# Series of small float32 products, whole and in column groups, after the last product of a two-layer hybrid model

## The chip, the cores and the metric

The kernel runs on one core of one Trainium2 chip. The core has five engines with queues of their own: TensorE (matrix products, its weight loads shown apart), VectorE (DVE), ScalarE (ACT), GpSimd (POOL) and SyncE (SP, which here issues most transfers). The metric is the device time of one execution in microseconds. The time before is the median of 2 runs, 1101.77 us; a profile was taken of one further execution.

## The reference

A model of two layers over 256 tokens of width 1024, with a memory of 256 tokens, all in float32. Each layer has four blocks, each closed by a layer normalization:

```python
for l in range(DEPTH):                      # 2
    h = layer_norm(ALPHA * h + 0.5 * swiglu(h, ffn1_gate[l], ffn1_up[l], ffn1_down[l]), ...)
    z = h @ w_in[l]
    cb, cc, ch, rq, rf, ri, rg, pu = jnp.split(z, split_at, axis=-1)
    y_conv = short_gated_conv(ch, cb, cc, conv_w[l])
    y_rec = hgrn2(rq, rf, ri, rg, lbs[l], rec_norm_g[l])
    y_pool = multiscale_pool(pu, pool_w[l], pool_scale[l])
    mix = jnp.concatenate([y_conv, y_rec, y_pool], axis=-1) @ w_out[l]
    h = layer_norm(ALPHA * h + mix, ...)
    h = layer_norm(ALPHA * h + cross_attn(h, mem, ca_q[l], ca_k[l], ca_v[l], ca_o[l]), ...)
    h = layer_norm(ALPHA * h + 0.5 * swiglu(h, ffn2_gate[l], ffn2_up[l], ffn2_down[l]), ...)
```

The two feed-forward blocks (1024 to 2816 and back) are most of the arithmetic. The change adds nothing to what is computed: the output is `h` after the second layer, as before.

## The kernel before

All data has 128 partitions. The tokens are two tiles of 128 (`NT = 2`), the width 1024 is eight tiles of 128 (`NK = 8`). The activations stand transposed in SBUF as `xT`, of shape 128 x 8 x 2 x 256: for each of the eight blocks of the width first the high parts of 256 tokens, then their low parts. `mT` is the same for the memory. Both are float32r, a form of float32 that TensorE multiplies in one pass with fewer bits. `split` (lines 60 to 62) makes high and low parts: ScalarE rounds a float32 tile to float32r, and VectorE subtracts that from the source. A product of float32 matrices is then three float32r products, high with high, high with low and low with high, all issued by `product` at line 106.

Weights come in blocks of 1 MB through `load` (line 76 issues the transfers on SyncE's queue) and are split the same way into `whi` and `wlo`.

Some smaller products use plain float32, not float32r: the blocks of the recurrence (lines 688, 711, 754, 764 and 765), the pooling's weights (line 816, 256 columns streamed) and the transposes by an identity (170, 254, 827, 888). At the start of the first feed-forward block, line 430 issues products of a zeroed tile into a PSUM tile `blank` that nothing reads; the helper `busy` is called with 5, 1 and 2.

PSUM has one pool with two tags, `acc` and `dn`, of four buffers each, one bank of 128 x 512 float32 a buffer. `acc(shape, tag)` takes the next buffer of a tag. A `dn` quadruple holds the four results (two token tiles, two halves of the width) of a block that returns to the width.

The last block is the second layer's `ffn(l, "ffn2", 3, ..., last=True)`. It ends in `finish`, which closes the two token tiles one after the other. For the second one the last half of the width is done in two pieces of 256 columns with an `acc` buffer each; VectorE adds a piece to `h` (line 309), takes statistics (317, 319, 321), GpSimd takes the power (322), VectorE normalizes (325, 329), and the output goes out from line 334 on the queues of SyncE and ScalarE. These steps follow the last matrix product of the program.

Most of the order of work is made by a planner that knows each engine's instructions and their dependencies. Inside `tc.manual_schedule(engines={...})` the named engines take their instructions in the order in which they are written. Line 966 of the profile is the end of the program, where SyncE waits for each engine and queue and all engines meet.

Of the kernel before, what the change touches and what calls it, by code (L numbers as in the profile page):

```python
# [8 lines left out]
F32 = mybir.dt.float32  # L9
# [5 lines left out]
E = mybir.EngineType  # L15
PSUM = bass.MemoryType.PSUM

P = 128
# [923 lines left out]
        pend = ffn(l, "ffn2", 3, pend, last=l == DEPTH - 1)  # L942


# [1 line left out]
_INS = [  # L946
    "x", "mem", "ffn1_gate", "ffn1_up", "ffn1_down", "w_in", "conv_w", "rec_lb", "rec_norm_g", "pool_w",
# [22 lines left out]
```

## Time and profile before

| what | us |
|---|---|
| time, median of 2 runs (1101.72 to 1101.82) | 1101.77 |
| the profiled execution, its time | 1101.39 |
| the profiled execution, from first to last instruction (span) | 1099.7 |
| VectorE busy | 834.5 |
| ScalarE busy | 566.2 |
| TensorE, products of line 106 with `whi` and `xT` into `acc`, 1312 of 512 columns | 394.9 |

The profile is of one execution. A row of the timeline gives start, length, engine (PE is a matmul, PEld a weight load, a q behind an engine its queue), source line, operation, output and inputs, shape and count; neighbouring instructions of one kind are merged, and the length then runs from the first start to the last end. Matmuls are pipelined: a row's recorded length is longer than the step from one start to the next. "128*128" are the rows and columns of the array that are used; "128x512" is the streamed operand. The shapes name both float32 and float32r as f32.

### The profile page before, as it was taken

The numbers are of one execution on the slowest core, as the hardware profiler recorded it, in microseconds if no ns is written. First come the engines' busy times: TensorE is split into PE (matmuls) and PEld (weight loads), VectorE is DVE, ScalarE is ACT, GpSimd is POOL, SyncE is SP. The second block draws the span as 40 slices with busy tenths as digits, with TensorE's granted clock in tenths as the row PEclk, the third lists the DMA queues.
The fourth block names the chain that finished last, engine by engine and source line by source line (L and its number), as shares of the span: only waits on it lengthen the run. The fifth ranks groups of instructions, "written<-read, shape, count | busy, mean of one in ns | idle before, by whom it ended". The sixth has DMA issues, their size and how long they took to land.

```text
span 1099.7 us, 14684 instructions
## 1 busy us (share of the span) xinstructions
PE 1089.5 (99%) x5667; PEld 968.6 (88%) x5667; DVE 834.5 (76%) x1089; ACT 566.2 (51%) x767; POOL 63.9 (6%) x112
## 2 busy tenths in 40 slices
PE   9999999999999999999999999999999999999997
PEld 7888888999899888888888888899998998888886
DVE  6678678998788777666687655699988877766665
ACT  6465454665457355444455445456564654554450
POOL 9600000000000000000000000000000000000000
PEclk9999999999999999999999999999999999999999
DMA  9987665744484396766488676656545645876651
GB/s 322 295 279 242 211 220 165 253 143 153 157 277 168 110 301 214 236 214 218 153 269 266 211 221 210 220 181 203 175 133 191 229 154 180 264 240 216 215 168 38
DMA packets 115749, 228.64 MB, mean 208 GB/s; under 512 B 5536, under 2 KB 38592, under 8 KB 110560
## 3 DMA queue, kind: packets, MB, share of 16 engines
q1 hardware_dynamic: 113888, 225.33, 62.9%
q0 software_dynamic: 1216, 1.20, 0.4%
q10 hardware_dynamic: 576, 1.18, 0.3%
q8 instruction: 44, 0.72, 0.3%
q14 instruction: 25, 0.20, 0.1%
HBM read 216.15 MB, written 1.05 MB: 198 GB/s over the span
## 4 chain that ended last, share of the span: by engine, by line
PE 98%; DVE 1%; issue 0%; DMA 0%; ACT 0%; DVEq 0%
PE acc L106 64%; PE dn L106 30%; PE acc L170 1%; PE dn L711 1%; DMA h<-in_x_dram 0%; PE dn L765 0%; PE dn L688 0%; DVE wlo L62 0%; PE dn L754 0%; PE dn L764 0%; PE dn L888 0%; PE acc L888 0%; DVE yr L772 0%; DVE h L329 0%; DVE h L325 0%
## 5 line engine op out<-in xcount | busy, mean ns | idle before, releaser
L62 DVE TENSOR_TENSOR wlo<-raw,whi 128x1024 fp32r<-128x1024 f32 (+1 forms) x396 | 474.1, 1212 | 187.7 <-ACT whi L61 176.2
L61 ACT CAST whi<-raw 128x1024 fp32r<-128x1024 f32 (+1 forms) x396 | 402.9, 1041 | 344.9 <-PE dn L106 160.1
L106 PE MATMUL acc<-whi,xT 128*128 128x512 f32 x1312 | 394.9, 379 | 0.0
L106 PEld LDWEIGHTS acc<-whi,xT 128*128 128x128 f32 x1312 | 247.8, 189 | 35.0
L106 PE MATMUL acc<-wlo,xT 128*128 128x512 f32 x656 | 248.6, 379 | 0.0
L106 PE MATMUL acc<-xT,whi 128*128 128x512 f32 x576 | 141.9, 382 | 0.0
L106 PEld LDWEIGHTS acc<-wlo,xT 128*128 128x128 f32 x656 | 124.0, 189 | 17.5
L106 PE MATMUL dn<-whi,ah 128*128 128x512 f32 x346 | 131.5, 380 | 0.0
L106 PE MATMUL dn<-wlo,ah 128*128 128x512 f32 x346 | 131.1, 379 | 0.0
L106 PE MATMUL dn<-whi,al 128*128 128x512 f32 x346 | 131.1, 379 | 0.0
L106 PEld LDWEIGHTS acc<-xT,whi 128*128 128x128 f32 x576 | 104.2, 190 | 11.2
L106 PE MATMUL dn<-whi,xT 128*128 128x512 f32 x288 | 88.2, 382 | 0.0
L106 PEld LDWEIGHTS acc<-xT,wlo 128*128 128x128 f32 x576 | 75.5, 191 | 3.9
L106 PE MATMUL acc<-xT,wlo 128*128 128x256 f32 x576 | 75.9, 275 | 0.0
L106 PEld LDWEIGHTS dn<-whi,al 128*128 128x128 f32 x346 | 65.4, 189 | 9.2
L106 PEld LDWEIGHTS dn<-wlo,ah 128*128 128x128 f32 x346 | 65.4, 189 | 9.2
L106 PEld LDWEIGHTS dn<-whi,ah 128*128 128x128 f32 x346 | 65.4, 189 | 9.2
L322 POOL TENSOR_TENSOR rs<-rs,nhalf 128x1 f32<-128x1 f32 x16 | 15.0, 935 | 855.5 <-DVE rs L321 855.5
L411 DVE STREAM_TRANSPOSE square<-dealt 128x512 f32<-128x512 f32 x40 | 63.4, 1656 | 0.5 <-DMA dealt<-sg 0.5
L106 PEld LDWEIGHTS dn<-whi,xT 128*128 128x128 f32 x288 | 54.4, 189 | 7.9 <-ACT whi L61 0.5
L106 PE MATMUL dn<-wlo,xT 128*128 128x512 f32 x144 | 54.8, 380 | 0.3 <-DVE wlo L62 0.3
L315 DVE SCALAR_TENSOR_TENSOR h<-h,dn 128x512 f32<-128x512 f32 x31 | 21.2, 684 | 33.9 <-PE dn L106 33.9
(204 smaller groups left out, 992.1 us busy)
## 6 DMA issues: line engine op xcount, KB each, us to landing
raw<-in_ffn_up_dram SPq DMA_DIRECT2D x44, 1024.0 KB, 5.1
raw<-in_ffn_down_dram SPq DMA_DIRECT2D x44, 1024.0 KB, 5.2
raw<-in_ffn_gate_dram SPq DMA_DIRECT2D x42, 1024.0 KB, 5.1
raw<-in_w_in_dram SPq DMA_DIRECT2D x24, 1024.0 KB, 5.0
dealt<-sg SPq DMA_DIRECT2D x80, 128.0 KB, 3.3
raw<-in_ca_k_dram SPq DMA_DIRECT2D x8, 1024.0 KB, 4.9
raw<-in_w_out_dram SPq DMA_DIRECT2D x8, 1024.0 KB, 4.9
raw<-in_ca_v_dram SPq DMA_DIRECT2D x8, 1024.0 KB, 5.1
```

The lines of the kernel that those rows point to most:

```text
L61: nc.scalar.copy(hi, src)
L62: nc.vector.tensor_tensor(lo, src, hi.bitcast(F32), op=ALU.subtract)
L106: nc.tensor.matmul(o, w, x, start=start, stop=stop)
L170: nc.tensor.transpose(pt[:, k, :], src[:, (4 * j + k) * P : (4 * j + k + 1) * P], unit)
L315: nc.vector.scalar_tensor_tensor(v, v, ALPHA / scale, sums(y[i][n]), op0=ALU.mult, op1=ALU.add)
L322: nc.gpsimd.tensor_tensor(rs, rs, nhalf[:, 0:1], op=ALU.pow)
L411: nc.vector.transpose(d.rearrange("p k (i b) -> p b k i", b=4), x[:, :, i, :].rearrange("p b (j k) -> p b k j", k=4))
L711: nc.tensor.matmul(o[:, hh], kc[:, hh, :], view(qf, hh * P + c, (other - c, 2), (2 * c, a), (1, c)), start=True, stop=True,)
```

## The change

Behind the loop over the layers three helpers and one block of hand-ordered TensorE work are added:

```diff
         pend = ffn(l, "ffn2", 3, pend, last=l == DEPTH - 1)
 
+    x1, m1 = (a.rearrange("p k h s -> p (k h s)") for a in (xT, mT))
+
+    def small(o, m, n, count, groups=None):
+        for i in range(count):
+            g = i % (P // m) if groups is None else groups[i % len(groups)]
+            w = x1[:, 512 * (i % 7) + m * g : 512 * (i % 7) + m * g + m].bitcast(F32)
+            x = m1[:, 512 * (i % 6) + n * g : 512 * (i % 6) + n * g + n].bitcast(F32)
+            nc.tensor.matmul(o[g * m : g * m + m, 0:n], w, x, start=True, stop=True)
+
+    def large(o, count, n=512):
+        for i in range(count):
+            x = m1[:, 512 * (i % 6) : 512 * (i % 6) + n]
+            nc.tensor.matmul(
+                o[:, 0:n], x1[:, 512 * (i % 7) : 512 * (i % 7) + P], x.rearrange("p (h c) -> p c h", h=2),
+                start=True, stop=True,
+            )
+
+    with tc.manual_schedule(engines={E.PE}):
+        o = acc((P, 512))
+        d = [acc((P, 512), "dn") for _ in range(2)]
+        large(o, 16)
+        small(o, 128, 128, 24)
+        small(o, 64, 64, 24)
+        small(o, 64, 64, 24, (0,))
+        small(o, 64, 128, 24)
+        small(o, 32, 32, 24)
+        small(o, 32, 64, 24)
+        small(o, 32, 128, 24)
+        small(o, 128, 64, 24)
+        small(o, 64, 64, 24)
+        for form in ((128, 128, 4), (64, 64, 8), (32, 32, 16), (64, 64, 16), (128, 64, 4)):
+            for r in range(4):
+                small(d[r % 2], *form)
+                large(o, 8)
+        large(o, 4)
+        large(o, 16, 256)
```

`small` multiplies `count` times. Each product loads `m` columns of the transposed activations as weights, all 128 rows deep, streams `n` columns of the transposed memory past them, and writes `m` partitions and `n` columns of PSUM. With `m` of 64 or 32 the products take turns among the two or four groups of `m` columns (group `g` writes partitions `g * m` onward); with `groups=(0,)` all stay in the first. Both operands are read as float32. `large` multiplies in float32r with 128 columns loaded and 512, or 256, streamed, as `product` does. In the text a small product of `m` loaded and `n` streamed columns is called m x n; nine series of 24 stand in a row, and then five forms are repeated four times each with eight large products behind every repetition. Nothing reads `o` or `d`, and every product starts its own sum.

## The prediction

> **What bounds the kernel now.** The page was read first: its engine table, then its chain that ended last.
>
> ```profile
> span 1099.7 us, 14684 instructions
> ...
> PE 1089.5 (99%) x5667; PEld 968.6 (88%) x5667; DVE 834.5 (76%) x1089; ACT 566.2 (51%) x767; POOL 63.9 (6%) x112
> ...
> PE 98%; DVE 1%; issue 0%; DMA 0%; ACT 0%; DVEq 0%
> ```
>
> TensorE is busy for 99% of the span and carries 98% of the chain. There is no idle TensorE time in mid-kernel that could take new products; what it leaves, 1099.7 - 1089.5 = 10.2 us, lies mostly behind its last product. So the end was read next, in the timeline, with the chain of waits in the same stretch (start, length, engine and line) and the rows of the last line of the program.
>
> ```profile
> 1079.98 8.20 PE dn L106 x38
> 1088.18 4.03 PE acc L106 x36
> ```
>
> ```profile
> 1091.82 0.19 PEld L106 LDWEIGHTS acc<-whi,al 128*128 128x128 f32 x1
> 1091.93 0.28 PE L106 MATMUL acc<-whi,al 128*128 128x256 f32 x1
> 1092.24 0.42 DVE L309 TENSOR_TENSOR h<-h,acc 128x256 f32<-128x256 f32 x1 [1.12 <-PE acc L106]
> ...
> 1096.02 0.35 ACTq L334 DMA_DIRECT2D out_dram<-h  x1
> ```
>
> ```profile
> L966 SPq EVENT_SEMAPHORE  x12: 17/28/28, 1096.8 to 1099.6; - x12
> ...
> L966 SPq DRAIN  x3: 7/7/7, 1098.8 to 1099.1; - x3
> L966 PEldq DRAIN  x2: 13/1106/2200, 1090.0 to 1099.2; - x2
> ```
>
> The last matrix product starts at 1091.93. Behind it come the last normalization on VectorE, the output's transfers, and from 1096.8 the closing waits of the sync queue, one per engine and queue, then drains and the end at 1099.7. TensorE's queue drains from 1090.0 for 2200 ns, so until 1092.2, and then waits for the others. The first closing drain of the sync queue is at 1098.8. If TensorE ends last, what follows it is this closing alone, 1099.7 - 1098.8 = 0.9 us.
>
> **The change, part by part.** It removes and moves nothing. It adds 408 small float32 products and 196 large float32r ones, in an order written by hand, on TensorE alone. No engine reads them, so nobody waits for them but the end of the program. Their inputs were finished long before. The nine rows that follow hold all prices: six of the timeline, two of the groups by shape and one of line 430.
>
> ```profile
> 215.51 1.95 PE L688 MATMUL dn<-q,k 128*128 128x128 f32 x16
> 217.22 0.46 PE L106 MATMUL acc<-whi,xT 128*128 128x512 f32 x1
> 217.51 0.38 PE L106 MATMUL acc<-wlo,xT 128*128 128x512 f32 x1
> ```
>
> ```profile
> 266.38 1.03 PE L816 MATMUL acc<-win,wpool 128*128 128x256 f32 x4
> ```
>
> ```profile
> 7.62 0.19 PEld L106 LDWEIGHTS dn<-wlo,xT 128*128 128x128 f32 x1 [0.62 <-DVE wlo L62]
> 7.62 0.48 PE L106 MATMUL dn<-wlo,xT 128*128 128x512 f32 x1 [0.32 <-DVE wlo L62]
> ```
>
> ```profile
> L688 PE MATMUL dn<-q,k 128*128 128x128 f32 x32 | 3.9, 275 | 0.0
> ...
> L816 PE MATMUL acc<-win,wpool 128*128 128x256 f32 x8 | 2.1, 379 | 0.0
> ```
>
> ```profile
> L430 PE MATMUL dn<-kTh x8: 396/628/796, 1.5 to 6.4; 128*128 128x512 f32 x8
> ```
>
> *How many instructions.* Line 688 issues 8 products per layer, 16 in both, and has 32 records: a float32 product is two pairs of a weight load and a matmul. So 408 small products are 816 pairs; a large float32r product is one.
>
> *Large products.* 512 columns: 8.20 / 38 = 0.2158 us. 256 columns: 4.03 / 36 = 0.112. There are 16 + 20 x 8 + 4 = 180 of the first and 16 of the second: 38.8 + 1.8 = 40.6 us.
>
> *Price of a small pair by its streamed columns.* At 128 columns line 688 gives (1.95 - 0.275) / 15 = 0.1117 us, at 256 line 816 gives (1.03 - 0.379) / 3 = 0.217 (a merged row runs from its first start to its last end, so one recorded length, 275 or 379 ns, comes off). The slope is 0.823 ns a column with 6.4 ns fixed; my estimate is 0.0591 us at 64 columns and 0.0327 at 32.
>
> *Price of a pair by its loaded columns.* No load of under 128 columns is in the trace. The product at 7.62 found the array empty: it lasted 0.48 where its kind lasts 0.38, so a bare load of 128 columns is about 0.10 to 0.11 us, close to the 0.1117 of the pair. In the stream that load costs nothing: the load at 1091.82 starts under a product still running, and the next product starts 0.11 later. For fewer columns the bounds are a load in proportion (0.055 us at 64, 0.0275 at 32) and one that doesn't shrink (0.11). I take the proportion, because the streaming side of the same array shows it, and so a pair costs by the larger of its two widths.
>
> *Sum.* Largest width 128: 40 products of 128x128, 24 each of 64x128 and 32x128, 40 of 128x64, together 128, so 256 pairs x 0.1117 = 28.6 us. Width 64: 168 of 64x64 (72 in the series, 32 + 64 in the repeated forms) and 24 of 32x64, so 384 x 0.0591 = 22.7. Width 32: 88 products, 176 x 0.0327 = 5.8. Small products: 57.1 us; with the large ones 97.7.
>
> *Switches.* Between series the kind of product changes 29 times to or from column groups. The nearest row is the change of type behind line 688: 16 pairs and one large product fill 217.51 - 215.51 = 2.00 us, and 16 x 0.1117 + 0.2158 is 2.003, so that change is free. The upper bound is a pipeline emptied each time, the recorded 0.275 less 0.112, plus a bare load of 0.11: 0.27 x 29 = 7.9 us. I take zero, by that row, and keep 8 for the range. [...]
>
> *Path.* The added work can start at 1091.93 + 0.11 = 1092.04; its PSUM buffers come from pools of four each whose older tiles were read before (the worst case, the one read by VectorE at 1092.24, would cost 0.6). The 6.8 us up to 1098.8 hide that much of it; the rest stands alone. Its last slot ends at 1092.04 + 97.7 = 1189.7, the matmul itself 0.16 later, and the closing adds 0.9: a span of 1190.8. The profiled execution took 1101.39 with a span of 1099.7, 1.7 more, and the median is 0.4 above it: **1193 us**, 8.3% slower.
>
> **The rivals.** *Column groups overlap* (chance 0.18). The code gives neighbouring products separate groups. If only their streams overlap and loads queue, the 64x128 and 32x64 series fall to the load's 0.0591 and 0.0327, and 32x128 to 0.0327: 48 x (0.0526 + 0.0264 + 0.079) = 7.6 us less, 1185. If loads overlap too, 288 pairs of 64x64 halve (8.5 less) and 176 of 32x32 fall to a quarter (4.3 less): 1172. For it: nothing forbids it; against: every row here uses all 128 columns, so none shows it. [...]
>
> *Loads of grouped products are not hidden* (0.14). Then a pair is load plus stream: 0.055 x (336 + 48) + 0.0275 x 272 = 28.6 more, 1221. Against: the load at 1091.82 is hidden. [...]
>
> *A pair has a flat price* (0.10), because the load does not shrink or instructions come no faster than a pair in 0.1117: 816 x 0.1117 = 91.1, 34 more, 1227. No row shows a shorter pair of this kind.
>
> *The clock falls* (0.06).
>
> ```profile
> 1092.20:1094.40 2.20, 0.00 (x1) 0.00 (x0) 2.06 (x6) 0.00 (x0) 0.65 (x1) 1.00 0.00 0
> 1094.50:1099.70 5.20, 0.00 (x0) 0.00 (x0) 1.88 (x4) 0.00 (x0) 0.17 (x1) 0.50 0.28 101
> ```
>
> In these stretches (first the length, then busy time of PE, PEld, DVE, ACT, POOL, then the granted clock) the clock halves 2.2 us after TensorE falls idle. If the nine series in a row, 34.4 us of small pairs, counted as idle, all but 2.2 us of them would double: 32 more, 1225. Against: the array works in each pair.
>
> *Each grouped product waits until the one before has landed* (0.06): 656 pairs then cost a load of 0.0275 or 0.055 and a whole recorded length, 0.275 at 128 columns and, along the line to 0.379 at 256, an estimated 0.223 at 64 and 0.197 at 32. That is 175 us in place of 39: 136 more, 1329. Against: at 128 columns a start comes every 0.1117 though each lasts 0.275.
>
> *The other side: nothing of it is executed* (0.02). If products without a reader are dropped when the program is built, TensorE still ends at 1092.2 and the time stays 1101.8. It decides only if nearly all goes, since with 2% of 1102 and the cover the work would have to cost under 6.8 + 22 = 29 us, less than the large products alone. Against: line 430's products into a buffer that nobody reads are called 5 + 1 + 2 = 8 times, and 8 are in the trace.
>
> **How the numbers follow.** My forecast has 0.42, with 1192 to 1201 by the switches; 0.02 is for what I don't see. The range of 1172 to 1228 takes in the forecast, the overlaps, unhidden loads, the flat price and the clock, 0.90 together, with the unknown prices of load and switch at its edges. It leaves out the full wait, the dropped products and the unseen. About 2%, 22 us, is what a measurement of this kernel can tell from no change. All cases but the dropped products are slower by more: 0.97 slower, 0.02 within, 0.01 faster for the unseen.
>
> **What would show it.** In the changed profile: two matmul records for each small product, starts 0.1117 apart in the 128-wide series, 0.059 at 64, 0.033 at 32, the alternating 64-wide series no faster than the one kept in one group; loads that start under the product before; 0.2158 between large products right behind a grouped series; granted clock 1.00 throughout; TensorE's last matmul about 0.9 us ahead of the end. Starts closer together in the alternating series would show the overlap, a step of 0.16 to 0.27 at a series' border the drain, a spacing of 0.11 at every width the flat price. An end near 1101.8 would make all of it wrong.

## The result, and the profile after

The changed kernel takes 1175.47 us against 1101.77: a ratio of 1.0672, with an interval of 1.0654 to 1.0689. That is slower, as forecast, and inside the range, but 17.5 us below the 1193 of the likeliest case, and close to the 1172 that stood as the fully overlapped form of the first rival. The profiled execution took 1175.47 with a span of 1173.8.

From the page after: the span, the engine table, and the chain of work that ended last by line (the changed lines are 954 for `small` and 959 for `large`).

```profile
span 1173.8 us, 16708 instructions
...
PE 1170.2 (100%) x6679; PEld 1041.4 (89%) x6679; DVE 834.6 (71%) x1089; ACT 566.9 (48%) x767; POOL 63.7 (5%) x112
...
PE acc L106 60%; PE dn L106 28%; PE acc L959 4%; PE acc L954 2%; PE dn L954 1%; PE acc L170 1%; PE dn L711 1%; PE dn L765 0%; PE dn L688 0%; DMA h<-in_x_dram 0%; DVE wlo L62 0%; PE dn L764 0%; PE dn L754 0%; PE dn L888 0%; PE acc L888 0%
```

TensorE has 6679 - 5667 = 1012 more matmuls, exactly 816 pairs and 196 large products. The other engines are as busy as before, VectorE for 834.6 us against 834.5.

The end of the program, now line 1006, in the rows of that line (each with count, shortest, median and longest in ns, first and last start):

```profile
L1006 SPq EVENT_SEMAPHORE  x12: 17/28/74172, 1096.8 to 1173.7; - x12
...
L1006 SPq DRAIN  x3: 7/7/7, 1172.9 to 1173.2; - x3
...
L1006 PEldq DRAIN  x2: 13/1209/2405, 1170.4 to 1173.3; - x2
```

The sync queue reaches its closing waits at 1096.8, as before, and then one of them lasts 74 us, in most of which TensorE alone works: from 1120.0 to 1172.5 it is busy for 52.50 us and VectorE, ScalarE and GpSimd for 0.00. TensorE drains until 1170.4 + 2.4 = 1172.8, the sync queue's first drain is at 1172.9, and the end comes 0.9 us later. So the added work lies on the path from the point at which the old tail no longer covers it.

What the price of a pair became is read in the timeline of TensorE, in five short stretches. The first four each hold a part of a series: 64x64 with two groups by turns, the same products in one group, 64x128 by turns, and 128x64. The fifth is one 32x32 form of 16 products in four groups.

```profile
1101.02 1.39 PE L954 MATMUL acc<-mT,xT 128*64 128x64 f32 x42
```

```profile
1102.83 1.39 PE L954 MATMUL acc<-mT,xT 128*64 128x64 f32 x21
```

```profile
1105.16 2.50 PE L954 MATMUL acc<-mT,xT 128*64 128x128 f32 x42
```

```profile
1110.81 4.41 PE L954 MATMUL acc<-mT,xT 128*128 128x64 f32 x38
```

```profile
1138.31 0.46 PE L954 MATMUL dn<-mT,xT 128*32 128x32 f32 x32
```

The first two rows have the same length and the same shape, and one has twice the matmuls of the other. With the recorded 0.222 us of the last one taken off, a pair costs (1.39 - 0.222) / 41 = 0.0285 us by turns and (1.39 - 0.222) / 20 = 0.0584 in one group. The third, with its recorded 0.274 off, gives 0.054, about half of what 128 streamed columns cost; the fourth, with 0.275 off, 0.1117, the same as with 128 streamed; the fifth (0.46 - 0.196) / 31 = 0.0085, a quarter of what 32 columns cost alone (0.032 in the one-group series of a later run).

The chain of waits around the repeated forms shows the second difference (start, length, what):

```profile
1125.60 0.89 PE dn L954 x8
1126.49 1.73 PE acc L959 x8
1128.22 0.61 PE dn L954 x16
1128.84 1.92 PE acc L959 x8
1130.76 0.61 PE dn L954 x16
```

The 128x128 form and its large products take 0.89 + 1.73 = 2.62 us, which is 8 x 0.1117 + 8 x 0.2158: no cost between them. The 64x64 form and its large products take 0.61 + 1.92 = 2.53, where 16 x 0.029 + 8 x 0.2158 is 2.19. A round trip from whole columns to groups and back costs 0.34 us.

### The profile page after: what moved, and what is told of

It is laid out like the page before. It is cut to its first block, busy times and chain, and to the rows that moved or that the text cites. A ratio compares the mean times of both kernels' runs of the same rounds, so it can differ in the third digit from the quotient of the medians.

```text
span 1173.8 us, 16708 instructions
## 1 busy us (share of the span) xinstructions
PE 1170.2 (100%) x6679; PEld 1041.4 (89%) x6679; DVE 834.6 (71%) x1089; ACT 566.9 (48%) x767; POOL 63.7 (5%) x112
## 4 chain that ended last, share of the span: by engine, by line
PE 99%; DVE 0%; issue 0%; DMA 0%; ACT 0%
PE acc L106 60%; PE dn L106 28%; PE acc L959 4%; PE acc L954 2%; PE dn L954 1%; PE acc L170 1%; PE dn L711 1%; PE dn L765 0%; PE dn L688 0%; DMA h<-in_x_dram 0%; DVE wlo L62 0%; PE dn L764 0%; PE dn L754 0%; PE dn L888 0%; PE acc L888 0%
## 5 line engine op out<-in xcount | busy, mean ns | idle before, releaser
L959 PE MATMUL acc<-mT,xT 128*128 128x512 f32 (+1 forms) x196 | 46.0, 381 | 0.0
```

Source lines behind the costliest of these rows:

```text
L959: nc.tensor.matmul(o[:, 0:n], x1[:, 512 * (i % 7) : 512 * (i % 7) + P], x.rearrange("p (h c) -> p c h", h=2), start=True, stop=True,)
```

## The experiments

Theory: products in different column groups run at the same time, loads and streams both (0.0285 us a pair by turns, 0.0584 in one group), and a change between whole and grouped columns has a price of its own (0.34 us a round trip). The rivals to it: a grouped product is cheap by its shape; the extra belongs to the start of a series; and, on how far the overlap reaches, three ideas of the queue. The last five kernels were timed once each.

### One group for all

```diff
-            g = i % (P // m) if groups is None else groups[i % len(groups)]
+            g = 0 if groups is None else groups[i % len(groups)]
```

> The change with one line altered: every grouped product loads and writes the first column group, none alternates; the number of products and their shapes stay. Theory A (pairs in different column groups run at the same time, load and stream both): without alternation a pair costs what the one-group 64x64 series costs in the changed kernel, 0.0584 us, and by the same slope 0.0327 for 32x32, 0.0591 for 32x64, about 0.110 for 64x128 and 32x128. That is 288 x 0.029 + 48 x 0.055 + 176 x 0.024 + 48 x 0.045 + 48 x 0.083 = 21.5 us more than the changed kernel: about 1197. Theory B (a grouped pair is cheap by its shape, and the one-group series is an exception of its own): about 1175.5, no change.

Measured: 1196.52 us, a ratio of 1.0864 (1.0832 to 1.0895). From its chain of waits, the same form as above:

```profile
1139.06 1.73 PE acc L959 x8
1140.79 1.08 PE dn L954 x16
1141.86 1.92 PE acc L959 x8
```

The 64x64 form lasts 1.08 us in place of 0.61; the large products behind it keep their 1.92. The shapes and the counts are the same, so shape does not set the price. Alternation among groups is worth 21 us of this change, as theory A said. The altered line moves the loaded columns, the streamed columns and the output partitions together, so this run doesn't tell which of the three has to differ.

### The large products gathered

```diff
             for r in range(4):
                 small(d[r % 2], *form)
-                large(o, 8)
+            large(o, 32)
```

> The change with the same products in another order: of each repeated form the four repetitions come first and their 32 large products after them, so that 9 of the 12 round trips between grouped and whole columns fall away. Theory A (a round trip between column modes costs 0.335 us, as the 64x64 and 32x32 forms with large products behind them show in the changed kernel against 16 or 32 pairs and 8 large products at their own steps): 9 x 0.335 = 3.0 us less than the changed kernel, 1172.5. Theory B (the extra belongs to the start of each call's series, whatever stands before it): 1175.5.

Measured: 1172.67 us (ratio 1.0647, 1.0616 to 1.0678). The interval overlaps that of the change, so the reading rests on the trace, whose span is 1171.1 against 1173.8, 2.7 less. From the chain:

```profile
1128.56 2.02 PE dn L954 x64
1130.57 7.10 PE acc L959 x32
```

Together 9.12 us, where 64 x 0.029 + 32 x 0.2158 = 8.76: one round trip of 0.36 us for four times the work. So the cost comes once with the change between whole and grouped columns, not with each call.

### How far the overlap reaches

The nine series and the repeated forms are replaced, so this kernel's time stands for itself:

```diff
+        for m, groups in (
+            (64, (0, 1)), (64, (0,) * 2 + (1,) * 2), (64, (0,) * 4 + (1,) * 4), (64, (0,) * 12 + (1,) * 12),
+            (32, (0,)), (32, (0, 1)), (32, (0, 2)), (32, (0, 1, 2, 3)), (32, (0, 0, 1, 1, 2, 2, 3, 3)),
+        ):
+            small(d[0], m, m, 48, groups)
+            large(o, 8)
```

> Other series in place of those of the change, each of 48 products (96 pairs) with 8 large products behind: 64x64 with groups in runs of 1, 2, 4 and 12 products, then 32x32 in one group, in groups 0 and 1, in 0 and 2, in all four by turns, and in all four in runs of 2. Theory A1 (each group has a short queue of some three pairs, filled in program order): series of 2.8, 2.9, 3.7, 5.1 us, then 3.2, 1.6, 1.6, 0.8, 0.9; time about 1139. Theory A2 (the engine looks some 32 pairs ahead): 2.8 four times, then 3.2, 1.6, 1.6, 0.8, 0.8; about 1136. Theory A3 (products start strictly in program order, only neighbours overlap): 2.9, 4.3, 5.0, 5.4, then 3.2, 1.6, 1.6, 1.6, 2.5; about 1145.

Measured: 1140.28 us. The timeline has one row for each series; the last is split by a pause.

```profile
1095.99 3.02 PE L954 MATMUL dn<-mT,xT 128*64 128x64 f32 x96
...
1100.87 3.07 PE L954 MATMUL dn<-mT,xT 128*64 128x64 f32 x96
...
1105.79 3.84 PE L954 MATMUL dn<-mT,xT 128*64 128x64 f32 x96
...
1111.48 5.28 PE L954 MATMUL dn<-mT,xT 128*64 128x64 f32 x96
...
1118.61 3.23 PE L954 MATMUL dn<-mT,xT 128*32 128x32 f32 x96
...
1123.69 1.71 PE L954 MATMUL dn<-mT,xT 128*32 128x32 f32 x96
...
1127.26 1.71 PE L954 MATMUL dn<-mT,xT 128*32 128x32 f32 x96
...
1130.82 1.03 PE L954 MATMUL dn<-mT,xT 128*32 128x32 f32 x96
...
1133.71 0.89 PE L954 MATMUL dn<-mT,xT 128*32 128x32 f32 x71
1134.99 0.47 PE L954 MATMUL dn<-mT,xT 128*32 128x32 f32 x25 [0.39 <-issue]
```

Less the last recorded length (0.22 or 0.20), the 64-wide series take 2.80, 2.85, 3.62 and 5.06 us: theory A1 said 2.8, 2.9, 3.7 and 5.1, theory A2 four times 2.8, theory A3 2.9, 4.3, 5.0 and 5.4. Without any overlap the 96 pairs would take 96 x 0.0584 = 5.6 us. So the overlap survives runs of two products in one group, is some 30% gone at four, and 80% gone at twelve. The estimates of theory A1 lie within 0.1 us of all four; its queue of some three pairs is not shown apart from these times. The 32-wide series show the divisor: 3.03 us in one group, 1.51 in two (0 with 1 and 0 with 2 alike), 0.83 in four. The last one takes 0.69 + 0.27 us without its pause, near the 0.9 of A1. A3 also falls on the eighth row: with two pairs for each product, strict order would give no more than two at once, 1.6 us. The changed kernel has a direct case, where the one-group 64x64 series hands over to 64x128. These rows count the matmuls of line 954 that run between 1105.0 and 1105.10, then between 1105.0 and 1105.11:

```profile
L954 PE MATMUL acc<-mT,xT x6: 222/222/322, 1104.8 to 1105.1; 128*64 128x64 f32 x5, 128*64 128x128 f32 x1
```

```profile
L954 PE MATMUL acc<-mT,xT x7: 222/222/322, 1104.8 to 1105.1; 128*64 128x64 f32 x6, 128*64 128x128 f32 x1
```

One 64x128 pair has started before the last 64x64 pair, which the code issues ahead of it.

The kernel is 1.3 us above the expected 1139. Its series hold a pause of 0.39 us marked "issue", for which the profile shows no wait, and the next run has a longer one, 1.17.

### No large products

All calls of `large` are left out.

> The change without its large products. Theory A (small and grouped products hold the granted clock as large ones do): the small products of the changed kernel take 80.6 - 40.6 = 40.0 us with all switches; 12 round trips go (4.0) and 4 single changes come (0.6): 36.6 us, so about 1131.5, with the granted clock at 1.00 until the end. Theory B (small products count as idle and the clock halves some 2.2 us after the last large one): all but 2.2 us of it doubles, about 1166.

Measured: 1133.13 us, with the granted clock at 1.00 over 38 us of small products alone (the clock stands behind the five engines' busy times):

```profile
1092.00:1130.00 38.00, 36.97 (x820) 35.91 (x819) 4.04 (x9) 0.00 (x0) 0.92 (x1) 1.00 0.05 17
```

The clock rival falls. The 1.6 us above the 1131.5 of theory A are mostly one pause, just behind the fast 32x32 forms, here in the timeline of the weight loads:

```profile
1121.10 0.62 PEld L954 LDWEIGHTS dn<-mT,xT 128*32 128x32 f32 x26
1122.88 0.43 PEld L954 LDWEIGHTS dn<-mT,xT 128*64 128x64 f32 x12 [1.17 <-issue]
```

### Long series

Is 0.0085 us a pair a rate, or only what a short burst shows?

```diff
         large(o, 16, 256)
+        large(o, 8)
+        small(o, 64, 64, 384)
+        large(o, 8)
+        small(o, 32, 32, 768)
```

> The change with two long series behind it: 8 large, 384 products of 64x64 in two groups by turns, 8 large, 768 of 32x32 in four groups by turns. Theory A (the short series' steps hold for any length): 768 pairs x 0.0292 = 22.4 us and 1536 x 0.0083 = 12.7, with 3.5 for the large ones and 0.5 for the changes of mode 39.1 more than the changed kernel: 1214.6. Theory B (instructions arrive in blocks of 16 KB, 128 pairs, and no faster than a block in about 2.3 us, as the 1.2 us pause behind the 32x32 products of the run without large products suggests): the 64x64 series is not touched, since its block lasts 3.7 us; the 32x32 series takes 12 blocks x 2.3 = 28 us: about 1230, with pauses on TensorE for which the profile shows no wait.

Measured: 1240.53 us, beyond both. The 64x64 series keeps its 0.0292, which the next fence shows first (timeline); the 32x32 series does not (same view; "issue" is idle time for which the profile shows no wait).

```profile
1174.24 22.62 PE L954 MATMUL acc<-mT,xT 128*64 128x64 f32 x768
```

```profile
1198.71 1.45 PE L954 MATMUL acc<-mT,xT 128*32 128x32 f32 x147
1200.60 1.28 PE L954 MATMUL acc<-mT,xT 128*32 128x32 f32 x128 [0.44 <-issue]
1204.06 1.59 PE L954 MATMUL acc<-mT,xT 128*32 128x32 f32 x128 [2.17 <-issue]
1207.52 1.93 PE L954 MATMUL acc<-mT,xT 128*32 128x32 f32 x128 [1.87 <-issue]
```

A burst starts every 3.46 us in these rows (1200.60, 1204.06, 1207.52), and each is 128 pairs, 256 instructions. The page counts what came over the instruction queue, first in the changed kernel, then here:

```profile
q8 instruction: 52, 0.85, 0.3%
```

```profile
q8 instruction: 70, 1.15, 0.4%
```

The 1152 products and 16 large ones added are 4 x 1152 + 2 x 16 = 4640 instructions, and 18 more packets came: some 258 instructions in each. The packets can be seen in the trace, too. In these windows the last column is what all transfers of the core moved, in GB/s:

```profile
1201.60:1201.80 0.20, 0.20 (x35) 0.17 (x21) 0.00 (x0) 0.00 (x0) 0.00 (x0) 1.00 0.30 82
1201.80:1205.10 3.30, 1.12 (x116) 1.04 (x109) 0.00 (x0) 0.00 (x0) 0.00 (x0) 0.94 0.00 0
1205.10:1205.30 0.20, 0.20 (x33) 0.20 (x26) 0.00 (x0) 0.00 (x0) 0.00 (x0) 0.50 0.30 82
1205.30:1208.70 3.40, 1.53 (x113) 1.40 (x108) 0.00 (x0) 0.00 (x0) 0.00 (x0) 0.50 0.00 0
```

82 GB/s in 0.20 us is 16.4 KB, one packet of the instruction queue (0.85 MB in 52), and nothing else is moved. Each packet starts 1.0 to 1.2 us into a burst, and the next burst follows 2.2 to 2.5 us behind it. So a block of some 256 arrives every 3.46 us, and that is 0.027 us a pair, where the pairs of the short bursts took 0.0085. Theory B had the blocks right and too small a price for them (2.3 us). TensorE is idle for 1.5 to 2.2 us between these bursts, as the chain of waits has it:

```profile
1201.89 2.17 issue
1204.06 1.59 PE acc L954 x95
1205.65 1.87 issue
1207.52 1.93 PE acc L954 x97
1209.45 1.53 issue
```

In this run the clock falls as well (same columns, the clock behind the five busy times):

```profile
1180.00:1200.00 20.00, 20.00 (x734) 19.44 (x729) 0.00 (x0) 0.00 (x0) 0.00 (x0) 1.00 0.02 4
1200.00:1210.00 10.00, 4.96 (x403) 4.47 (x389) 0.00 (x0) 0.00 (x0) 0.00 (x0) 0.74 0.02 5
1210.00:1220.00 10.00, 5.80 (x384) 5.40 (x384) 0.00 (x0) 0.00 (x0) 0.00 (x0) 0.50 0.02 5
```

Over the window that holds the pause of 2.17 us the clock is still 0.94, behind it 0.50, and a burst stretches from 1.28 us to 1.93. That costs nothing here: the next burst starts 1.53 us after its end. The next run has almost as much idle time and keeps its clock.

### Long series, wider

```diff
-        small(o, 64, 64, 384)
+        small(o, 32, 128, 768)
         large(o, 8)
-        small(o, 32, 32, 768)
+        small(o, 32, 64, 768)
```

> As the long run, with 768 products of 32x128 in place of the 64x64 ones and 768 of 32x64 in place of the 32x32 ones. Theory A (steps hold for any length): 1536 pairs x 0.0273 = 41.9 us and 1536 x 0.0142 = 21.8, with 4.0 for the rest 67.7 more than the changed kernel: 1243.2. Theory B (no faster than a block of 128 pairs in about 2.3 us): 32x128 is not touched (3.5 us a block), 32x64 takes 12 x 2.3 = 28 us: 1249.

Measured: 1262.37 us. The timeline:

```profile
1174.43 42.68 PE L954 MATMUL acc<-mT,xT 128*32 128x128 f32 x1536
```

```profile
1221.58 1.99 PE L954 MATMUL acc<-mT,xT 128*32 128x64 f32 x128 [0.30 <-issue]
1225.32 1.99 PE L954 MATMUL acc<-mT,xT 128*32 128x64 f32 x128 [1.75 <-issue]
1229.07 1.99 PE L954 MATMUL acc<-mT,xT 128*32 128x64 f32 x128 [1.75 <-issue]
```

32x128 in four groups (the first row) takes (42.68 - 0.27) / 1535 = 0.0276 us a pair without a pause, close to the 0.027 at which instructions came in the run before. 32x64 takes (1.99 - 0.22) / 127 = 0.014 within a burst, and its bursts start 3.74 and 3.75 us apart. Theory A falls; theory B is again right in kind, with the price of the run before, not 2.3. TensorE idles for almost half of this series, too, yet the clock stays at 1.00:

```profile
1221.50:1259.50 38.00, 21.48 (x1389) 19.86 (x1389) 0.00 (x0) 0.00 (x0) 0.00 (x0) 1.00 0.02 5
```

The pauses in its rows are of 0.30 and 1.75 us, and the clock fell behind one of 2.17; whether the length of the pause decides is not shown.

### The same fast products, spaced

```diff
         large(o, 16, 256)
+        for r in range(12):
+            small(d[r % 2], 32, 32, 64)
+            large(o, 16)
```

> The change with the 768 products of 32x32 of the long run behind it, but in 12 parts of 64 products (128 pairs, as many as a block of instructions holds) with 16 large products behind each part. Theory C (instructions arrive no faster than a block of 256 in about 3.5 us, and what arrives early waits in store; only a demand above that rate costs): a part and its large products take 128 x 0.0085 + 16 x 0.2158 + 0.335 = 4.88 us, while their 288 instructions need 3.9 us to arrive, so there is no pause: 58.5 us more than the changed kernel, 1234. Theory D (every 128 fast pairs are followed by a pause of their own of some 1.8 us, whatever the demand): 12 x 1.8 = 21.6 us more, 1256.

Measured: 1233.70 us. The 768 products that took 38.9 us in one series (the span of 1238.8 less 1198.71, the closing of 1.0 and a last length of 0.2) are busy for 15.6 us here, with no idle TensorE time ahead of any (the group's row, then one part of 128 pairs in the timeline, unbroken):

```profile
L954 PE MATMUL dn<-mT,xT 128*32 128x32 f32 x1536 | 15.6, 198 | 0.0
```

```profile
1177.31 1.30 PE L954 MATMUL dn<-mT,xT 128*32 128x32 f32 x128
```

So a burst of 128 pairs runs at 0.0087 us a pair with no pause behind it when 16 large products follow: the parts start 4.87 us apart (1172.44 and 1177.31), and at the long run's rate their 288 instructions would need an estimated 288 / 256 x 3.46 = 3.9. Theory D falls. That a pause of the long run waits for its instructions is read from the packets there, one ahead of each burst.

## Why the prediction was right, and where it was not

The sign and the range held. The case that came was not that of the forecast (0.42) but that of the first rival (0.18), with a price for the switches that the forecast put at nothing. These two errors have opposite signs, so that the forecast is off by no more than 17.5 us is in part luck. By its own steps:

- **Path: right.** The first large product follows the last old one with the ordinary step (1091.90 to 1092.01, 0.11 us), the closing after TensorE's end is the 0.9 us that the forecast took, and no other engine moved. The end of the program waits 74 us for TensorE alone.
- **Number of pairs, large products, load of 128 columns: right.** 1012 new matmuls, 0.2158 us for a large one, 0.1117 for a pair with 128 loaded columns, streamed 128 or 64.
- **Price by width in one group: right.** 0.0584 us at 64 columns for the estimated 0.0591, 0.032 at 32 for 0.0327. The bound of a load that doesn't shrink was not needed.
- **"A pair costs by the larger of its two widths": wrong where groups take turns**, and this is the step that failed. It took the array as one place, since every row before used all 128 columns. Pairs whose neighbours are in other groups came cheaper: 288 pairs of 64x64 at 0.029 (0.0584 in one group), 48 of 64x128 at 0.054, and the 32-wide series, timed in the long and short runs, at 0.0085, 0.014 and 0.0276 for 32, 64 and 128 streamed columns. Against the forecast's prices that is 8.7 + 2.8 + 4.3 + 2.2 + 4.0 = 22.0 us less. The run with one group puts 21 of them back. The rival had named this with a chance of 0.18 and 20.4 us in its full form, in which it left 64x128, 32x64 and 32x128 at the price of loads that queue.
- **Switches "I take zero": wrong.** The change of type behind line 688 was not the right neighbour, because both sides of it use whole columns. A round trip costs 0.34 us; 12 of them and five single changes, taken as half of that each, make 4.9 us. That is 0.17 us a change, at the low end of the step of 0.16 to 0.27 that the prediction named as the sign of a drain, and the run with gathered products agrees. What is measured is the price; that the engine empties meanwhile is not shown apart from it.
- The two add up: 97.7 - 22.0 + 4.9 = 80.6 us of added work, and from the first large product to the end of the last slot the trace has 80.6. With the rest of the sum as it stood this is 1175.8, and 1175.47 was measured.
- **The clock: right** in the changed kernel, 1.00 to the end. Of the runs with added work, only the long one with 32x32 has less than 1.00 (0.50 late in that series, 0.986 as the mean of the run).
- **Unhidden loads, the flat price, the full wait and the dropped products: none came.** In one group a pair costs 0.0584 us at 64 columns and 0.032 at 32, no more than the prediction's estimates for its streamed columns alone (0.0591 and 0.0327), so no load adds to it there, nor at 128 columns with 0.1117.

## What to carry to other kernels

Small float32 products that filled only a part of the columns cost by their own width when all stood in the same column group (0.0584 us a pair at 64x64, 0.032 at 32x32), and by about that width over the number of groups when neighbours alternated (0.029 in two groups, 0.0085 in four); order them so that the group changes every product or two, since runs of four in two groups of 64 already lost some 30% of the gain. Keep grouped products together: each excursion from whole columns cost 0.34 us, as much as 12 alternating pairs of 64x64. And in a long series count instructions before columns: of 32x32 and 32x64, whose pairs took 0.0085 and 0.014 us within a burst, no more than 128 pairs came in 3.46 and 3.74 us, 0.027 and 0.029 a pair.

## What was unexpected

TensorE reached 0.0085 us a pair, two instructions, in bursts, where no pair before was shorter than 0.11 us. It did not start products strictly in program order across column groups, as the four-group series (0.83 us where theory A3, strict order, said 1.6) and the start of the 64x128 series (one pair ahead of the last 64x64 pair) show. And the supply of instructions, a block of 256 in 3.46 us in the 32x32 series and 3.74 in the 32x64 one, bounded a kernel of straight code. The profile puts that idle time down to "issue"; what it is was read from the packets of the instruction queue, 16.4 KB ahead of each of two bursts.
